# Gate and up projections of a feed-forward layer by seven half products instead of eight, with weight sums formed by accumulating loads

## The chip, the cores and the metric

The kernel runs on one core of a Trainium2 chip. The metric is the device time of one execution in microseconds (us). Three runs of the kernel before took 2762.12, 2761.25 and 2759.31 us; their median, 2761.25 us, is the time before.

## The reference

A trunk of two layers works on 512 tokens of width 1024. Each layer is a half-step feed-forward block, a token mixer with four branches, and a second half-step feed-forward block, each between two RMS norms:

```
def swiglu(h, w_gate, w_up, w_down):
    return (jax.nn.silu(h @ w_gate) * (h @ w_up)) @ w_down
...
for l in range(DEPTH):
    f = swiglu(rms_norm(h, ffn1_pre_g[l]), ffn1_w_gate[l], ffn1_w_up[l], ffn1_w_down[l])
    h = h + FFN_RESIDUAL_SCALE * rms_norm(f, ffn1_post_g[l])
    u = rms_norm(h, mix_pre_g[l])
    ...
    h = h + rms_norm(merged @ w_o[l], mix_post_g[l])
    f = swiglu(rms_norm(h, ffn2_pre_g[l]), ffn2_w_gate[l], ffn2_w_up[l], ffn2_w_down[l])
    h = h + FFN_RESIDUAL_SCALE * rms_norm(f, ffn2_post_g[l])
```

D_FF is 2816, so gate and up are each 1024 x 2816. All values are float32.

## The kernel before

**Numbers in two parts.** Every matrix operand is cut into a high part (a cast to float32r) and a low part (the rest), and a product of two such operands is three matmuls, high by high, high by low and low by high: `mm3` (L128 to L132) where a 128x128 block of weights is the stationary operand, `by_tokens` (L219 to L221) where the tokens are.

**The weights.** All weights lie in DRAM in one stream `ws`, in the order of their use, in chunks of eight 128x128 blocks (512 KB). `load` (L91 to L102) brings a chunk: a DMA on SP's queue into `raw` (3 buffers), ScalarE's cast to `wh` (L100), VectorE's subtraction to `wl` (L101). `block` hands out the next block of the stream and sees to it that the AHEAD = 3 chunks behind it are asked for.

**A feed-forward block.** `boundary` (L235) ends the block before and begins this one. It runs the last projection of the block before (down or output projection, tokens as stationary operand, result `py` in PSUM), and for each 128 tokens `gained` (squares on ScalarE, L233; product with the gain, L299), `update` (the residual stream `h`, held in SBUF, L304) and `normed` (squares, a power on GpSimd, L229; scaling to `u`, L250). `turned` transposes `u` (L262) and cuts it into `xh` and `xl` (L153, L146), for 256 tokens at a time. As soon as the first 256 tokens are there, `outer` multiplies them with 32 blocks of weights, two gate columns and two up columns (a column is 128 of the 2816 outputs) into four banks of PSUM `pf`; then the second 256 tokens follow with the same blocks. A third pair of columns is done by `group` (eight `mm3` of all 512 tokens in one bank).

`ffn` (L355) then takes each of the 22 column pairs: silu of gate (ScalarE, L361), times up (VectorE, L366), cut into `gh` and `gl` (L151, L144). The columns from the fourth on are dense: 8 blocks times 3 matmuls of 512 tokens for gate, and the same for up.

```
for f in range(3, KF):
    x = gate(group([(f"ffn{n}_w_gate", l, k, f * P) for k in range(KD)], xs))
    up(group([(f"ffn{n}_w_up", l, k, f * P) for k in range(KD)], xs), x)
```

**What sets the order.** Every engine works through its own instructions in order, and each has one queue of them. The kernel's order of calls, and the buffers that its pools have (8 banks of PSUM, 5 chunks each of `wh` and `wl`, 59 slots of 128x512 in SBUF), decide what stands where.

Of the kernel before, what the change touches and what calls it, by code (L numbers as in the profile page):

```python
# [9 lines left out]
F32 = mybir.dt.float32  # L10
F32R = mybir.dt.float32r
# [4 lines left out]
P = 128  # L16
# [22 lines left out]

PACE = (3, 1, 5)  # L40

HOLD = 8

_VECS = ("ffn1_pre_g", "mix_pre_g", "ffn2_pre_g", "a_conv_w", "b_conv_w", "b_conv_b", "b_ln_g", "b_ln_b", "c_subln_g")
# [10 lines left out]
def build(tc, ws, x, vecs, gains, wdf, lamv, fb, consts, out):  # L55
# [2 lines left out]
    order = []  # L58
    with ExitStack() as ctx:
        cp = ctx.enter_context(tc.tile_pool(name="cp", bufs=1))  # L60
        sp = ctx.enter_context(tc.tile_pool(name="sp", bufs=59))
        rawp = ctx.enter_context(tc.tile_pool(name="rawp", bufs=3))
        wp = ctx.enter_context(tc.tile_pool(name="wp", bufs=5))
        mp = ctx.enter_context(tc.tile_pool(name="mp", bufs=4))
        np_ = ctx.enter_context(tc.tile_pool(name="np", bufs=4))
        gp = ctx.enter_context(tc.tile_pool(name="gp", bufs=1))
# [21 lines left out]

        ready = {}

        def load(c, parts=1):  # L91
# [12 lines left out]
        def block(desc):  # L104
            i = len(order)
            order.append(desc)
            if i % CB == 0:
                c = i // CB
                for n in range(c, min(c + AHEAD + 1, NBLK // CB) if len(order) > 4 * KD else 0):
                    if n not in ready:  # L110
# [14 lines left out]
            for _ in range(min(pace[0], len(spare))):  # L125
                spare.pop(0)()

        def mm3(out, w, x, first, last):  # L128

            PE.matmul(out=out, lhsT=w[0], rhs=x[0], start=first, stop=False)  # L130
            PE.matmul(out=out, lhsT=w[0], rhs=x[1], start=False, stop=False)  # L131
            PE.matmul(out=out, lhsT=w[1], rhs=x[0], start=False, stop=last)  # L132

        def group(descs, xs):
            out = ps()
# [99 lines left out]
        def boundary(post, pre, first):  # L235
# [2 lines left out]


            xs, pf, blk = [], [], []  # L240
            stat = np_.tile([P, 16], F32, tag="stat", name=nm("stat"))

            def normed(t):

                for c in range(2):
                    squares(hs[t][c], stat[:, 8 + 2 * t + c:9 + 2 * t + c])
                r = rstd_of([stat[:, 8 + 2 * t + c:9 + 2 * t + c] for c in range(2)])
                us = [slot(F32, "u") for _ in range(2)]
                for c in range(2):
                    V.tensor_scalar(out=us[c], in0=hs[t][c], scalar1=r, scalar2=None, op0=ALU.mult)  # L250
                return us

            def turned(us, h):

                c = HALVES[h]
                for b in range(4):
                    p = ps("pt")
                    for i in range(2):
                        k = 2 * b + i
                        for t in range(2):  # L260
                            o = k % 4 * P
                            PE.transpose(out=p[:, i * H + t * P:i * H + (t + 1) * P],  # L262
                                         in_=us[t][k // 4][:, o:o + P], identity=ident)
                    for i in range(2):
                        k = 2 * b + i
# [4 lines left out]
                        lo_of(xs[k][1][:, c], p[:, i * H:(i + 1) * H], xs[k][0][:, c], g)  # L270

            def outer(k, c):

# [9 lines left out]
            if post is None:  # L283
                for t in range(4):
                    for c in range(2):
                        nc.sync.dma_start(out=hs[t][c], in_=x[t * P:(t + 1) * P, c * T:(c + 1) * T])
                    load(t, 2 if t == 0 else 1)
                us = [normed(t) for t in range(4)]
            else:
                row, factor, name, l, ys = post  # L290
                n = len(ys)
                gb = gp.tile([P, D], F32, tag="gb", name=nm("gb"))
                nc.scalar.dma_start(out=gb, in_=gains[row:row + 1, :].broadcast_to([P, D]))
                yg = [[None, None] for _ in range(4)]

                def gained(t, c, p):
                    squares(p, stat[:, 2 * t + c:2 * t + c + 1])
                    yg[t][c] = slot(F32, "yg")
                    V.tensor_mul(out=yg[t][c], in0=p, in1=gb[:, c * T:(c + 1) * T])  # L299
# [10 lines left out]
                settle()  # L310
                py = [ps("py") for _ in range(4)]
                for k in range(n):
                    w = tile4(name, l, k, 0)
# [23 lines left out]
                    return None  # L337
            if post is None:
                turned(us[0:2], 0)
            for k in range(KD - 2):  # L340
                outer(k, HALVES[0])
            turned(us[2:4], 1)
            for k in range(KD - 2, KD):
                outer(k, HALVES[0])
            for k in range(KD):
                outer(k, HALVES[1])
            pf.append(group(first[4], xs))
            pf.append(group(first[5], xs))
            return xs, pf


        def ffn_first(l, n):
            return [[(f"ffn{n}_w_{w}", l, k, f * P) for k in range(KD)] for f in range(3) for w in ("gate", "up")]

        def ffn(l, n, entry):  # L355
            xs, pf = entry
            gs = []

            def gate(pg):
                x = slot()  # L360
                S.activation(out=x, in_=pg, func=AF.Silu)  # L361
                return x

            def up(pu, x):
                u = slot()
                V.tensor_mul(out=u, in0=pu, in1=x)  # L366
                gs.append(split(u, s="g"))

            for f in range(3):
                x = gate(pf[2 * f])  # L370
                up(pf[2 * f + 1], x)
# [3 lines left out]
            settle()  # L375
            return 3 * l + 2 * n - 2, 0.5, f"ffn{n}_w_down", l, gs


        def cols(l, c0):
# [5 lines left out]
        def mixer(l, entry):  # L385
            lam_init = 0.8 - 0.6 * math.exp(-0.3 * l)
            xs, pf = entry

            def proj(c0):
                return group(cols(l, c0), xs)  # L390
# [357 lines left out]

        vec = cp.tile([P, NCOLS], F32, name="vec")
        nc.scalar.dma_start(out=vec, in_=vecs)  # L750
        hs = [[cp.tile([P, T], F32, name=f"h{t}{c}") for c in range(2)] for t in range(NQ)]
# [15 lines left out]
        qlo, nq = [[cp.tile([P, T], F32R, name=f"qlo{i}{m}") for m in range(2)] for i in range(2)], [0]  # L767
        for pair in qlo:
            for m in range(2):
                V.memset(pair[m][LANES[1 - m]].bitcast(F32), 0.0)  # L770
        mhalf = cp.tile([P, 4], F32, name="mhalf")
        V.memset(mhalf, -0.5)

# [67 lines left out]
```

## Time and profile before

| | |
|---|---|
| median of 3 runs | 2761.25 us (2759.31 to 2762.12) |
| the profiled execution | 2762.7 us, of which the span of its records is 2760.9 us |
| mean granted clock of TensorE | 0.995 |
| busy | TensorE matmuls 2717.1 us, VectorE 1392.6, ScalarE 980.1, GpSimd 71.5 |

The span is the time from the first to the last record; the rest of the execution's time lies around it. The profile has a line per engine of how busy it was, the chain of work that ended last, groups of like instructions with their mean duration, a timeline with the start of every instruction, and windows, which sum up a stretch. A row of the timeline or of the groups begins with the engine and the line of the source. TensorE appears twice: PE for matmuls and PEld for the loading of their stationary operand. The busy time of a matmul overlaps with that of the next, so the pace of matmuls is read from the distance of their starts and not from their duration.

### The profile page before, as it was taken

The numbers are of one execution on the slowest core, as the hardware profiler recorded it, in microseconds if no ns is written. First come the engines' busy times: TensorE is split into PE (matmuls) and PEld (weight loads), VectorE is DVE, ScalarE is ACT, GpSimd is POOL, SyncE is SP. The second block draws the span as 40 slices with busy tenths as digits, with TensorE's granted clock in tenths as the row PEclk, the third lists the DMA queues.
The fourth block names the chain that finished last, engine by engine and source line by source line (L and its number), as shares of the span: only waits on it lengthen the run. The fifth ranks groups of instructions, "written<-read, shape, count | busy, mean of one in ns | idle before, by whom it ended". The sixth has DMA issues, their size and how long they took to land.

```text
span 2760.9 us, 32249 instructions
## 1 busy us (share of the span) xinstructions
PE 2717.1 (98%) x12884; PEld 2274.7 (82%) x12884; DVE 1392.6 (50%) x2287; ACT 980.1 (35%) x1607; POOL 71.5 (3%) x114
## 2 busy tenths in 40 slices
PE   7999999999999999999999999999999999999998
PEld 6888888887888888888888888888878888888887
DVE  4333248777776453332353332596777854533322
ACT  4222232354454333222242222424545533432221
POOL 0000000000000000000000000000000000000000
PEclk9999999999999999999999999999999999999999
DMA  4222223222222222222222222222222222222221
GB/s 154 99 96 95 100 82 111 85 77 69 96 81 92 99 92 99 92 99 100 84 101 99 99 94 98 95 98 79 75 85 88 87 93 94 90 100 99 99 92 69
DMA packets 73494, 257.82 MB, mean 93 GB/s; under 512 B 8432, under 2 KB 8816, under 8 KB 73344
## 3 DMA queue, kind: packets, MB, share of 16 engines
q1 hardware_dynamic: 68688, 246.45, 25.7%
q10 hardware_dynamic: 4656, 9.32, 1.1%
q8 instruction: 101, 1.65, 0.2%
q14 instruction: 49, 0.40, 0.0%
HBM read 253.60 MB, written 2.13 MB: 93 GB/s over the span
## 4 chain that ended last, share of the span: by engine, by line
PE 95%; DVE 2%; ACT 1%; issue 1%; DMA 1%; POOL 1%; POOLq 0%; DVEq 0%; ACTq 0%
PE p L130 21%; PE p L132 21%; PE p L131 21%; PE py L219 6%; PE py L220 6%; PE py L221 6%; PE pf L131 2%; PE pf L132 2%; PE pf L130 2%; PE o L548 1%; PE pv L219 1%; PE pv L220 1%; PE pv L221 1%; PE pt L532 1%; PE sc L502 1%; DVE wl L101 1%
## 5 line engine op out<-in xcount | busy, mean ns | idle before, releaser
L100 ACT CAST wh<-raw 128x1024 fp32r<-128x1024 f32 (+1 forms) x465 | 488.7, 1051 | 1400.7 <-PE p L131 663.5
L101 DVE TENSOR_TENSOR wl<-raw,wh 128x1024 fp32r<-128x1024 f32 (+1 forms) x465 | 567.9, 1222 | 753.2 <-ACT wh L100 741.4
L130 PE MATMUL p<-xh,wh 128*128 128x512 f32 x2304 | 903.5, 392 | 0.0
L132 PE MATMUL p<-xh,wl 128*128 128x512 f32 x2304 | 898.4, 390 | 0.0
L131 PE MATMUL p<-xl,wh 128*128 128x512 f32 x2304 | 898.0, 390 | 0.0
L132 PEld LDWEIGHTS p<-xh,wl 128*128 128x128 f32 x2304 | 433.2, 188 | 90.8
L131 PEld LDWEIGHTS p<-xl,wh 128*128 128x128 f32 x2304 | 433.7, 188 | 89.1 <-issue 0.5
L130 PEld LDWEIGHTS p<-xh,wh 128*128 128x128 f32 x2304 | 433.8, 188 | 88.7 <-PE pt L532 0.5
L219 PE MATMUL py<-wh,gh 128*128 128x512 f32 x704 | 274.1, 389 | 0.0
L221 PE MATMUL py<-wh,gl 128*128 128x512 f32 x704 | 273.9, 389 | 0.0
L220 PE MATMUL py<-wl,gh 128*128 128x512 f32 x704 | 273.9, 389 | 0.0
L366 DVE TENSOR_TENSOR s<-p,s 128x512 f32<-128x512 f32 x80 | 55.3, 692 | 270.9 <-PE p L132 270.9
L395 DVE SCALAR_TENSOR_TENSOR yc<-ba,vec,yc 128x501 f32<-128x501 f32 (+17 forms) x240 | 170.0, 733 | 2.4
L221 PEld LDWEIGHTS py<-wh,gl 128*128 128x128 f32 x704 | 132.2, 188 | 27.6
L219 PEld LDWEIGHTS py<-wh,gh 128*128 128x128 f32 x704 | 132.2, 188 | 27.5
L220 PEld LDWEIGHTS py<-wl,gh 128*128 128x128 f32 x704 | 132.2, 188 | 27.1
L131 PE MATMUL pf<-xl,wh 128*128 128x256 f32 x384 | 112.8, 295 | 8.8 <-DVE xl L146 8.8
L130 PE MATMUL pf<-xh,wh 128*128 128x256 f32 x384 | 109.7, 296 | 4.4 <-ACT xh L153 3.1
L132 PE MATMUL pf<-xh,wl 128*128 128x256 f32 x384 | 112.2, 294 | 0.0
L522 ACT ACTIVATE e<-e,mx 128x128 f32<-128x128 f32 (+3 forms) x128 | 71.4, 558 | 66.1 <-DVE mx L520 54.4
L131 PEld LDWEIGHTS pf<-xl,wh 128*128 128x128 f32 x384 | 77.9, 203 | 10.1 <-DVE xl L146 10.1
L130 PEld LDWEIGHTS pf<-xh,wh 128*128 128x128 f32 x384 | 74.8, 200 | 7.9 <-ACT xh L153 5.6
(185 smaller groups left out, 2617.8 us busy)
## 6 DMA issues: line engine op xcount, KB each, us to landing
raw<-ws SPq DMA_DIRECT2D x463, 512.0 KB, 3.2
cb<-cum ACTq DMA_DIRECT2D x16, 256.0 KB, 3.5
gb<-gains ACTq DMA_DIRECT2D x6, 512.0 KB, 3.7
h<-x SPq DMA_DIRECT2D x8, 256.0 KB, 5.8
out<-h SPq DMA_DIRECT2D x4, 256.0 KB, 2.0
out<-h ACTq DMA_DIRECT2D x4, 256.0 KB, 2.0
raw<-ws SPq DMA_DIRECT2D x2, 256.0 KB, 7.1
cst<-consts ACTq DMA_DIRECT2D x1, 384.0 KB, 4.7
```

The source lines that it names most:

```text
L100: S.copy(out=wh[:, j], in_=raw[:, j])
L101: V.tensor_sub(out=wl[:, j], in0=raw[:, j], in1=wh[:, j].bitcast(F32))
L130: PE.matmul(out=out, lhsT=w[0], rhs=x[0], start=first, stop=False)
L131: PE.matmul(out=out, lhsT=w[0], rhs=x[1], start=False, stop=False)
L132: PE.matmul(out=out, lhsT=w[1], rhs=x[0], start=False, stop=last)
L219: PE.matmul(out=out, lhsT=x[0][:, r], rhs=w[0], start=first, stop=False)
L220: PE.matmul(out=out, lhsT=x[0][:, r], rhs=w[1], start=False, stop=False)
L221: PE.matmul(out=out, lhsT=x[1][:, r], rhs=w[0], start=False, stop=last)
L366: V.tensor_mul(out=u, in0=pu, in1=x)
L395: V.scalar_tensor_tensor(out=acc[:, s:], in0=y[:, :T - s], scalar=vcol(wname, l, i * 4 + j), in1=acc[:, s:], op0=ALU.mult, op1=ALU.add)
L502: PE.matmul(out=p[:, :n], lhsT=q[0][m][:, c], rhs=k[m][:, :n], start=True, stop=False)
L522: S.activation(out=e, in_=e, func=AF.Exp, scale=-1.0, bias=mx, accum_out=sums)
```

## The change

**Seven products for eight.** Of each feed-forward block, two column pairs stay as they were (through `outer`); the third, dense pair goes. The other 20 column pairs are taken in 10 groups (GROUPS) of two pairs. For gate and for up apart, the two columns (rows of the output) by 8 blocks of weights and by 512 tokens are seen as a 2x2 matrix of weights (a11, a12, a21, a22: two columns by the upper and lower four blocks of the 1024) times a 2x2 matrix of activations (b11 ... b22: upper and lower four blocks by the two halves of the tokens). By Strassen's scheme in Winograd's form the product takes seven products of sums instead of eight products: a12 b21, a11 b11, s1 nt1, s2 nt2, s3 t3, a22 t4 and s4 b22. Each is 4 blocks x 3 matmuls of 256 tokens, for gate and for up.

**The sums of weights.** `seven` (new, L466) loads the four quarters of a group. s1 to s4 are made by DMAs on GpSimd's queue that add to what lies in SBUF: `add` (L483). X receives s1, s2 and s4 in turn (three additions), Y receives s3 (one); Z and W are a12 and a22 as they are. An addition can begin when the cut of the sum before (cast and subtraction, `cut`, L104 and L105) has read the buffer. `raw` has 7 buffers now.

**The sums of activations.** In `boundary`, ScalarE keeps `xf`, the uncut second half (L294), GpSimd puts the first half together again from `xh` and `xl` (`whole`, L301), and VectorE makes nt1, nt2, t3 and t4 from them (`quarter_sums`, L417), each cut in two (`form`, L161 to L170).

**The sums of products.** Products add up in PSUM in banks f0 and f1. What two outputs share is copied out by ScalarE (`taken`, L499) and added by VectorE (`added`, L504).

**Residual stream in DRAM.** `normed` stores `h` by DMAs on ScalarE's queue (L268), and `fetch` reads gain and `h` back in the middle of the next projection (L330, L333). The cut of `g` in two parts moves from `ffn` into that projection (`part`). `qlo` is allotted and set to zero in each mixer.

```diff
-        sp = ctx.enter_context(tc.tile_pool(name="sp", bufs=59))
-        rawp = ctx.enter_context(tc.tile_pool(name="rawp", bufs=3))
+        sp = ctx.enter_context(tc.tile_pool(name="sp", bufs=65))
+        rawp = ctx.enter_context(tc.tile_pool(name="rawp", bufs=7))
...
             def normed(t):
                 for c in range(2):
                     squares(hs[t][c], stat[:, 8 + 2 * t + c:9 + 2 * t + c])
+                    if post is not None:
+                        nc.scalar.dma_start(out=hd[t][c], in_=hs[t][c])
...
+                    for i in range(2 if sums and h else 0):
+                        S.activation(out=xf[b][h][:, i * H:(i + 1) * H], in_=p[:, i * H:(i + 1) * H], func=AF.Copy,
+                                     scale=vcol(pre[0], pre[1], 2 * b + i))
...
             turned(us[2:4], 1)
...
+            for k in range(KD):
+                outer(k, HALVES[1])
+                if k == 0:
+                    nt1 = quarter_sums(ALU.subtract, b11, b12)
+                    form("nt1", nt1)
+                if k == 2:
+                    t2 = quarter_sums(ALU.add, b22, nt1)
+                    form("nt2", t2, True)
+                if k == 4:
+                    form("t3", quarter_sums(ALU.subtract, b22, b12))
+                if k == 6:
+                    form("t4", quarter_sums(ALU.subtract, t2, b21))
+                if k < 6:
+                    next(steps)
+            return steps, pf
...
+            def add(g, key, u):
+                G.dma_start(out=ga[g][key], in_=ws[base + 4 * g + u], accum_op=ALU.add)
...
+            def product(g, name, to, x, first):
+                wh, wl = ga[g].pop(name)
+                for i in range(2):
+                    for k in range(4):
+                        c = slice(i * T + k * P, i * T + (k + 1) * P)
+                        mm3(to[i], (wh[:, c], wl[:, c]), forms[x][k], first and k == 0, k == 3, True)
...
+                if r == -1:
+                    split_of(g, "a12", "Z")
+                    split_of(g, "s1", "X")
+                    add(g, "X", 0)
+                if r == 0:
+                    split_of(g, "a11", "Y")
+                    add(g, "Y", 2)
+                if r == 3:
+                    split_of(g, "s2", "X")
+                    add(g, "X", 1)
+                if r == 5:
+                    split_of(g, "s3", "Y")
...
+                if r == 2:
+                    d["f1"] = [ps("f1") for _ in range(2)]
+                    product(g, "a11", [p[:, HALVES[0]] for p in d["f1"]], "b11", True)
+                    taken(g, "n1")
+                    added(g, *[[p[:, HALVES[0]] for p in d["f0"]]] * 2, "n1")
+                if r == 3:
+                    product(g, "s1", [p[:, HALVES[1]] for p in d["f0"]], "nt1", True)
...
         def ffn(l, n, entry):
-            for f in range(3, KF):
-                x = gate(group([(f"ffn{n}_w_gate", l, k, f * P) for k in range(KD)], xs))
-                up(group([(f"ffn{n}_w_up", l, k, f * P) for k in range(KD)], xs), x)
+            steps, pf = entry
+            for f in range(2):
+                up(pf[2 * f + 1], gate(pf[2 * f]))
+            for t in steps:
...
```

**Where instructions stand.** Of two tensors with the same name, the number behind the underscore tells them apart; the rest of a row is line, operation, output, inputs and shape. ScalarE, before, where the second feed-forward block of the first layer begins; the first silu (L361) is the one that frees a bank `pf`:

```order
L153 ACTIVATE xh_8054<-pt_8225,vec 128x256
L153 ACTIVATE xh_8067<-pt_8234,vec 128x256
L153 ACTIVATE xh_8080<-pt_8243,vec 128x256
L100 CAST wh_8187<-raw_8186 128x1024
L100 CAST wh_8253<-raw_8252 128x1024
L100 CAST wh_8380<-raw_8379 128x1024
L361 ACT_TABLE_LOAD
L361 ACTIVATE s_8440<-pf_8122 128x512
L100 CAST wh_8411<-raw_8410 128x1024
L151 CAST gh_8444<-s_8442 128x512
```

Three casts of weights stand between the last cut of activations and the table load.

The same place now; `th` are the high parts of the sums of activations, `wh_9679` is s2, `wh_9713` s3, `wh_9746` and `wh_9750` a12 and s1 of the second group:

```order
L104 CAST wh_9679<-raw_9471 128x1024
L170 ACTIVATE th_9508<-t_9501 128x512
L104 CAST wh_9713<-raw_9512 128x1024
L168 CAST th_9542<-t_9538 128x512
L104 CAST wh_9746<-raw_9709 128x1024
L168 CAST th_9546<-t_9539 128x512
L104 CAST wh_9750<-raw_9677 128x1024
L168 CAST th_9592<-t_9588 128x512
L168 CAST th_9596<-t_9589 128x512
L452 ACT_TABLE_LOAD
L452 ACTIVATE s_9612<-pf_9297 128x512
L452 ACTIVATE s_9616<-pf_9299 128x512
```

The table load and the first silu (L452 now) stood behind three casts of weights; they now stand behind the cuts of all four sums of activations and of s2, s3 and the next group's first two.

TensorE now, at the end of a11's product of the first group (f_9647). f_9789 is the first bank of the second group, the ninth bank to be asked for; f_9646 gets s2, f_9620 s1:

```order
L149 MATMUL f_9647<-xh_9219,wl_9572 128x256
L147 MATMUL f_9789<-xh_9228,wh_9746 128x256 [waits PE_49,Activation_49]
L148 MATMUL f_9789<-xl_9229,wh_9746 128x256
L149 MATMUL f_9789<-xh_9228,wl_9747 128x256 [waits DVE_49]
L147 MATMUL f_9789<-xh_9232,wh_9746 128x256
L147 MATMUL f_9646<-th_9504,wh_9679 128x256 [waits Activation_49]
L148 MATMUL f_9646<-tl_9505,wh_9679 128x256
L149 MATMUL f_9646<-th_9504,wl_9680 128x256
L147 MATMUL f_9646<-th_9504,wh_9679 128x256
L147 MATMUL f_9620<-th_9463,wh_9554 128x256 [waits DVE_49]
```

The first product of the second group stands ahead of s2 and s1 of the first, and its first matmul waits for ScalarE.

GpSimd now, at the same boundary; nr_9281 is the power for the last 128 tokens, raw_9471 is X, raw_9512 Y:

```order
L246 TENSOR_TENSOR nr_9281<-nw_9280,mhalf 128x1
L301 TENSOR_TENSOR xf_8832<-xh_9202,xl_9203 128x256
L301 TENSOR_TENSOR xf_8832<-xh_9206,xl_9207 128x256
L301 TENSOR_TENSOR xf_8834<-xh_9215,xl_9216 128x256
L301 TENSOR_TENSOR xf_8834<-xh_9219,xl_9220 128x256
L301 TENSOR_TENSOR xf_8836<-xh_9228,xl_9229 128x256
L301 TENSOR_TENSOR xf_8836<-xh_9232,xl_9233 128x256
L301 TENSOR_TENSOR xf_8838<-xh_9241,xl_9242 128x256
L301 TENSOR_TENSOR xf_8838<-xh_9245,xl_9246 128x256
L483 DMA raw_9471<-ws 128x1024
L483 DMA raw_9512<-ws 128x1024
L483 DMA raw_9471<-ws 128x1024
```

The second addition to X (raw_9471, which makes s2) and the one to Y stand behind the eight additions that put `xf` together.

## Rows read from the trace of the kernel before

**Rows 1.** The page: share of the span by engine, and the chain of work that ended last.

```profile
PE 2717.1 (98%) x12884; PEld 2274.7 (82%) x12884; DVE 1392.6 (50%) x2287; ACT 980.1 (35%) x1607; POOL 71.5 (3%) x114
...
PE 95%; DVE 2%; ACT 1%; issue 1%; DMA 1%; POOL 1%; POOLq 0%; DVEq 0%; ACTq 0%
```

**Rows 2.** Windows, inside the first feed-forward block: the stretch, its length, then busy time and instructions of each engine, granted clock, share of the DMA engines.

```profile
110.00:340.00 230.00, 230.00 (x1016) 190.51 (x1015) 73.59 (x78) 63.63 (x81) 0.00 (x0) 1.00 0.28 96
```

**Rows 3.** Timeline of TensorE there: start, duration. Between the two rows lie 25 more matmuls of this form.

```profile
199.25 0.39 PE L130 MATMUL p<-xh,wh 128*128 128x512 f32 x1
...
205.14 0.39 PE L132 MATMUL p<-xh,wl 128*128 128x512 f32 x1
```

**Rows 4.** Timeline of TensorE, matmuls of 256 tokens in `outer`: 50 more lie between the first two rows, 9 between the last two.

```profile
405.62 0.29 PE L132 MATMUL pf<-xh,wl 128*128 128x256 f32 x1
...
411.73 0.28 PE L132 MATMUL pf<-xh,wl 128*128 128x256 f32 x1
...
1026.32 0.41 PE L132 MATMUL pf<-xh,wl 128*128 128x256 f32 x1
...
1028.45 0.41 PE L130 MATMUL pf<-xh,wh 128*128 128x256 f32 x1
```

**Rows 5.** Groups of like instructions on VectorE and ScalarE: busy time in all, mean ns of one, then idle time before them.

```profile
L101 DVE TENSOR_TENSOR wl<-raw,wh 128x1024 fp32r<-128x1024 f32 x463 | 566.5, 1224 | 750.4 <-ACT wh L100 738.6 <-PE pt L532 0.8 <-PE st L188 0.3
L100 ACT CAST wh<-raw 128x1024 fp32r<-128x1024 f32 x463 | 487.5, 1053 | 1397.1 <-PE p L131 663.5 <-issue 337.7 <-PE py L221 314.2
L569 DVE TENSOR_TENSOR s<-s,s 128x512 f32<-128x512 f32 x48 | 33.1, 690 | 1.2
L366 DVE TENSOR_TENSOR s<-p,s 128x512 f32<-128x512 f32 x80 | 55.3, 692 | 270.9 <-PE p L132 270.9
L144 DVE TENSOR_TENSOR gl<-s,gh 128x512 fp32r<-128x512 f32 x88 | 59.6, 685 | 0.0
L144 DVE TENSOR_TENSOR pl<-pt,ph 128x256 fp32r<-128x256 f32 x24 | 10.0, 415 | 0.0
L151 ACT CAST ph<-pt 128x256 fp32r<-128x256 f32 x24 | 9.1, 378 | 6.0 <-PE pt L532 6.0
L151 ACT CAST gh<-s 128x512 fp32r<-128x512 f32 x88 | 54.7, 621 | 3.5 <-DVE s L366 3.5
L361 ACT ACTIVATE s<-p 128x512 f32<-128x512 f32 x80 | 47.0, 588 | 0.0
L361 ACT ACT_TABLE_LOAD x3 | 3.8, 1283 | 0.1
```

**Rows 6.** DMA queues (packets, MB, share of 16 engines' span) and issues (count, KB each, median us from issue to landing); in the last row, of SP's issues, the shortest, median and longest ns of one.

```profile
q1 hardware_dynamic: 68688, 246.45, 25.7%
...
raw<-ws SPq DMA_DIRECT2D x463, 512.0 KB, 3.2
cb<-cum ACTq DMA_DIRECT2D x16, 256.0 KB, 3.5
...
L99 SPq DMA_DIRECT2D raw<-ws x465: 327/328/432, 1.7 to 2712.9; - x155
```

**Rows 7.** Timeline at the boundary before the second feed-forward block of the first layer: start, duration, in brackets the idle time before and what ended it.

```profile
1024.13 0.39 PE L131 MATMUL pf<-xl,wh 128*128 128x256 f32 x1 [1.47 <-DVE xl L146]
...
1034.01 0.55 POOL L229 TENSOR_TENSOR nr<-nw,mhalf 128x1 f32<-128x1 f32 x1 [2.60 <-DVE nw L228]
...
1036.75 2.67 ACT L153 ACTIVATE xh<-pt,vec 128x256 fp32r<-128x256 f32 x7 [3.07 <-PE pt L262]
...
1037.45 0.36 PE L130 MATMUL pf<-xh,wh 128*128 128x256 f32 x1
...
1040.89 0.48 DVE L146 SCALAR_TENSOR_TENSOR xl<-pt,vec,xh 128x256 fp32r<-128x256 f32 x1 [0.54 <-ACT xh L153]
...
1048.79 1.28 ACT L361 ACT_TABLE_LOAD   x1
1050.08 0.60 ACT L361 ACTIVATE s<-pf 128x512 f32<-128x512 f32 x1
```

**Rows 8.** Windows of that boundary, columns as in rows 2: behind the wait of TensorE, and the last stretch of `outer`.

```profile
1026.10:1028.60 2.50, 2.50 (x13) 2.50 (x13) 1.52 (x4) 1.61 (x4) 0.00 (x0) 0.50 0.64 228
1037.40:1049.00 11.60, 11.60 (x99) 11.60 (x98) 5.91 (x11) 5.84 (x11) 0.00 (x0) 1.00 0.21 66
```

**Rows 9.** Groups on GpSimd, columns as in rows 5.

```profile
L512 POOL CAST ph<-zeros 128x128 fp32r<-128x128 f32 x24 | 15.4, 640 | 565.5 <-DVE s L448 206.7 <-PE o L548 101.5 <-DVE s L569 74.6
L577 POOL CAST w8s<-zeros 128x192 fp32r<-128x192 f32 x2 | 1.1, 546 | 0.0
```

More of the change, by code (lines that the diff above doesn't have):

```diff
@@ L89, in build, with cut @@
         ready = {}
+        apart = set()
+        for l in range(DEPTH):
+            for n in range(2):
+                c = (2 * FFN_CHUNKS + MIX_CHUNKS) * l + (FFN_CHUNKS + MIX_CHUNKS) * n + PLAIN
+                apart.update(range(c, c + 4 * GROUPS))
+        def cut(raw):
+            wh = wp.tile([P, CB * P], F32R, tag="wh", name=nm("wh"))
+            wl = wp.tile([P, CB * P], F32R, tag="wl", name=nm("wl"))
+            S.copy(out=wh, in_=raw)
+            V.tensor_sub(out=wl, in0=raw, in1=wh.bitcast(F32))
+            return wh, wl
         def load(c, parts=1):
@@ L109, in block @@
                 for n in range(c, min(c + AHEAD + 1, NBLK // CB) if len(order) > 4 * KD else 0):
-                    if n not in ready:
+                    if n not in ready and n not in apart:
                         load(n)
@@ L126, in cover, with mm3 @@
                 spare.pop(0)()
[L128 to L132, printed above, removed]
+        def mm3(out, w, x, first, last, free=False):
+            PE.matmul(out=out, lhsT=w[0], rhs=x[0], start=first, stop=False, skip_group_check=free)
+            PE.matmul(out=out, lhsT=w[0], rhs=x[1], start=False, stop=False, skip_group_check=free)
+            PE.matmul(out=out, lhsT=w[1], rhs=x[0], start=False, stop=last, skip_group_check=free)
         def group(descs, xs):
@@ L240, in boundary @@
             xs, pf, blk = [], [], []
+            sums = pre is not None and pre[0] != "mix_pre_g"
+            xf = [[slot(F32, "xf") for _ in range(2)] for _ in range(4)] if sums else None
+            hs = [[None, None] for _ in range(NQ)]
             stat = np_.tile([P, 16], F32, tag="stat", name=nm("stat"))
@@ L291, in boundary, with fetch, part @@
                 n = len(ys)
-                gb = gp.tile([P, D], F32, tag="gb", name=nm("gb"))
-                nc.scalar.dma_start(out=gb, in_=gains[row:row + 1, :].broadcast_to([P, D]))
+                gb = []
+                def fetch():
+                    for c in range(2):
+                        gb.append(slot(F32, "gb"))
+                        nc.scalar.dma_start(out=gb[c], in_=gains[row:row + 1, c * T:(c + 1) * T].broadcast_to([P, T]))
+                        for t in range(NQ):
+                            hs[t][c] = slot(F32, "h")
+                            nc.scalar.dma_start(out=hs[t][c], in_=hd[t][c] if row else
+                                                x[t * P:(t + 1) * P, c * T:(c + 1) * T])
+                def part(k):
+                    if k < n and not isinstance(ys[k], tuple):
+                        ys[k] = halves(ys[k])
                 yg = [[None, None] for _ in range(4)]
@@ L342, in boundary, with form, quarter_sums @@
             turned(us[2:4], 1)
+            if not sums:
+                for k in range(KD - 2, KD):
+                    outer(k, HALVES[0])
+                for k in range(KD):
+                    outer(k, HALVES[1])
+                pf.append(group(first[4], xs))
+                pf.append(group(first[5], xs))
+                return xs, pf
+            forms, t2 = {}, [None, None]
+            def form(name, srcs, negate=False):
+                out = []
+                for src in srcs:
+                    hi, lo = slot(F32R, "th"), slot(F32R, "tl")
+                    hi_of(hi, src, -1.0 if negate else None)
+                    lo_of(lo, src, hi, -1.0 if negate else None)
+                    out.extend((hi[:, i * H:(i + 1) * H], lo[:, i * H:(i + 1) * H]) for i in range(2))
+                forms[name] = out
+            def quarter_sums(op, a, b):
+                out = [slot(F32, "t") for _ in range(2)]
+                for i in range(2):
+                    V.tensor_tensor(out=out[i], in0=a[i], in1=b[i], op=op)
+                return out
+            b11, b12, b21, b22 = ([xf[b + 2 * r][h] for b in range(2)] for r in range(2) for h in range(2))
+            for j, k in enumerate(range(4)):
+                forms.setdefault("b11", []).append(tuple(v[:, HALVES[0]] for v in xs[k]))
+                forms.setdefault("b21", []).append(tuple(v[:, HALVES[0]] for v in xs[k + 4]))
+                forms.setdefault("b22", []).append(tuple(v[:, HALVES[1]] for v in xs[k + 4]))
+            steps = seven(first[0][0][0], first[1][0][0], first[0][0][1], forms)
             for k in range(KD - 2, KD):
@@ new lines, in boundary @@
+                if k == 2:
[8 more added lines that the diff above has]
+            return steps, pf
+        def ffn_first(l, n):
+            return [[(f"ffn{n}_w_{w}", l, k, f * P) for k in range(KD)] for f in range(2) for w in ("gate", "up")]
@@ new lines, in build, with gate, up, halves @@
+        gs = []
+        def gate(pg, scale=1.0):
+            x = slot()
+            S.activation(out=x, in_=pg, func=AF.Silu, scale=scale)
+            return x
+        def up(pu, x, scale=1.0):
+            u = slot(F32, "g")
+            V.scalar_tensor_tensor(out=u, in0=pu, scalar=scale, in1=x, op0=ALU.mult, op1=ALU.mult)
+            gs.append(u)
+        def halves(src):
+            hi, lo = slot(F32R, "gh"), slot(F32R, "gl")
+            hi_of(hi, src)
+            lo_of(lo, src, hi)
+            return hi, lo
@@ new lines, in ffn @@
+        def ffn(l, n, entry):
+            steps, pf = entry
+            for f in range(2):
+                up(pf[2 * f + 1], gate(pf[2 * f]))
+            for t in steps:
+                if t == 7 * GROUPS - 2:
+                    for k in range(AHEAD):
+                        gs[k] = halves(gs[k])
+                if t >= 7 * GROUPS + 2 and t % 2:
+                    c = len(order) // CB + (t - 7 * GROUPS - 2) // 2
+                    load(c)
+            ys = gs[:]
+            gs.clear()
+            return 3 * l + 2 * n - 2, 0.5, f"ffn{n}_w_down", l, ys
@@ L387, in mixer @@
             xs, pf = entry
+            qlo, nq = [[slot(F32R, "ql") for m in range(2)] for i in range(2)], [0]
+            for pair in qlo:
+                for m in range(2):
+                    V.memset(pair[m][LANES[1 - m]].bitcast(F32), 0.0)
             def proj(c0):
@@ L766, in build @@
         V.memset(zeros, 0.0)
[L767 to L770, printed above, removed]
         mhalf = cp.tile([P, 4], F32, name="mhalf")
```

96 lines of the change are left out of this document (74 added, 22 removed).

## The prediction

> **What bounds the kernel now.** I read the page first: PE is busy 98% of the span and makes up 95% of the chain, VectorE stands at 50%, ScalarE at 35% [rows 1]. So a stage gets shorter only if PE gets less to do there, and whatever makes PE wait costs its full length. Then the windows: in the middle of a feed-forward block PE has no gap in 230 us, VectorE works 73.6 us and ScalarE 63.6, and the DMA engines 28% [rows 2]. The timeline gives the pace of matmuls: with 512 tokens 26 starts in 5.89 us, 0.2265 us each [rows 3]; with 256 tokens 51 starts in 6.11 us, 0.1198 each, and 10 in 2.13 us, 0.213 each, where the clock is low [rows 4].
>
> **What PE saves.** Two dense column pairs were 96 matmuls of 512 tokens, 96 x 0.2265 = 21.75 us. A group is now 7 products x 2 x 4 blocks x 3 matmuls = 168 of 256 tokens, 168 x 0.1198 = 20.13 us. That is 1.62 us less for each of 10 groups in 4 blocks: **-64.8 us**. Seven for eight would be 2.72 us; a matmul of half the tokens takes 53% of the time, which eats 1.1 of it.
>
> **Where a group could be held up.** The cuts of seven chunks cost VectorE 7 x 1.224, the six copies' additions 6 x 0.415 and two products of some 0.69, 12.4 us in all; ScalarE 7 x 1.053 + 6 x 0.378 + 2 x 0.588 = 10.8 us [rows 5]. Both fit in 20.1 us. What counts is order. s1 adds to f0, and may start only when VectorE has added the copy of a11's first bank. That bank is ready 12 matmuls, 1.44 us, before a11 ends; the copy (0.378) and the addition (0.415) fit, unless ScalarE and VectorE are at s4's cut (1.053 and 1.224) then. With five buffers of `wh` a cast starts when the fifth before it has been used; s4's starts 2.9 us before a11 ends, and the addition is done 0.15 us before PE wants it. So the bounds of this wait are 0 and 1.6 us (all four in a row, less 1.44) per group.
>
> The weight sums are the other holder. A plain load of 512 KB keeps the 16 DMA engines for 25.7% x 2760.9 us x 0.524 / 246.45 = 1.51 us, and lands 3.2 us after its issue [rows 6]. An accumulating load isn't in the trace. It brings as many bytes, so 1.51 us is its lower bound; twice the landing time of a load, 6.4 us, is the upper one, if it first fetches what lies there and then goes over it again. I take twice a load, 3.0 us, as the row of one load is the nearest. A group then needs 4 x 1.51 + 4 x 3.0 = 18 us of DMA engines, of 20.1. The tightest sum is s2's: the next s1's cast may start when a22 has been used, 11.5 us into a group, its cut ends at 13.8, and s2's cast is due when s3 has been used, at 20.2; so 6.4 us are left for waiting on GpSimd, issue and landing. I put landing at 3.2 + 1.5 = 4.7 us and the issue at 0.3 (SP's, rows 6) to 1.7 us (a wide guess: three of GpSimd's small casts, rows 9). That just fits, so I take 0.3 us per group for both holders together, **+12 us**, bounds 0 and 1.6 x 40 = 64.
>
> [...]
>
> **The fill at each feed-forward block.** This is the largest loss I see. `outer`'s second half starts at 1037.45, its 96 matmuls take 11.5 us [rows 7, 8]; a12 and a11 add 2 x 24 x 0.12 = 5.8. So PE has work for 17.3 us. Its next instruction wants a ninth bank, which the first silu frees. Before, that silu stood behind three casts, ended at 1050.7, 13.2 us in [rows 7], and the dense third pair (48 x 0.2265 = 10.9 us) covered it. Now it stands behind the cuts of all the activation sums. VectorE gets to these when the last `xl` is done: 1041.4 before [rows 7], now after six copies of `xf` on ScalarE (0.378 each) at about 1042.6, 5.2 us in. Until the last of t4's sums it has 8 sums (0.690), 5 cuts of weights (1.224) and 6 low parts (0.685): 15.8 us [rows 5], so 21.0 us in. Then a high part (0.62), the table load (1.283) and silu (0.588): **23.5 us in, 6.2 us after PE ran dry**. Lower bound: even with VectorE out of the way, the cast ahead of it (the next group's s1) needs a11's buffer, free at 17.3, so silu comes 4.2 us late. On top, s2's addition stands on GpSimd behind eight additions of 128 x 256. These start at 1034.6 [rows 7]; GpSimd's cast of 128 x 128 took 0.64 and 128 x 192 0.55 [rows 9], so I put one at 1.3 us (bounds 0.6, and 2.6 for twice the width and two inputs), done 7.6 us in; the sum then lands 13 us in, about 1 us after VectorE could use it. [...] Together 6.2 + 0.3 for handovers + 1 + 1.5 = 9 us, four times: **+36 us** (bounds 17, from 4.2 each, and 78, with 2.6 us an addition). The first block, which has no projection ahead of it, I take like the others.
>
> [...]
>
> **The small parts.** In the first half of each such boundary a fifth chunk (a12) is cut between the `xh` and `xl` that PE waits for: 1.2 us of VectorE, four times, **+5** (0 to 10). `normed` issues eight stores on ScalarE at five boundaries; at 0.33 us an issue [rows 6] only the last group's count, **+2** (0 to 13). The loads of gain and `h`, ten on ScalarE, and the cuts of `g`, 22 x 0.62 on ScalarE and 22 x 0.685 on VectorE, lie in the down projection, where PE has 59.8 us of matmuls (264 x 0.2265) for its first half alone: nothing. Zeroing `qlo` lies in the mixer, nothing. The last products of a block alternate on PE with the down projection's first: nothing, at most 1 us each.
>
> **Sum.** 2762.7 - 64.8 + 12 + 36 + 5 + 2 = 2752.9 us for an execution like the profiled one, which lies 1.45 above the median: **2751.5 us**, 0.35% faster. I take 0.2%, 5.5 us, as what a measurement can tell.
>
> **Rivals.** (A) *The fill is at its lower bound* and groups run without a wait: 2762.7 - 64.8 + 17 - 1.4 = 2714 us. For it: VectorE is half idle there before [rows 8], and a sum that lands early costs nothing. Against it: 15.8 us of VectorE's own durations don't shrink. (B) *The sums are late in every group*, the case on the other side. From 6.7 us between the end of s1's cut and landing, each further us costs 1 us in each of 40 groups, since ScalarE and VectorE stand in order behind the waiting cast, s1's addition among the rest. At 8 us it is 1.6 x 40 = 64 where I took 12: 2803. The same place with another cause: above (20.1 - 6.0) / 4 = 3.5 us of engine time per accumulating load the DMA engines become the bound, and at 4.5 us a group takes 24.0 us, 2.3 more than before, and the kernel 2761 + 40 x 2.3 + 43 = 2896. For it: 90% load of the DMA engines by my own estimate, and 6.4 us against 5 to 6.4; against it, the rows have no accumulating load that is slow. (C) *GpSimd's additions take 2.6 us each*: they end 18 us in, s2's sum lands 23 in, silu comes 10 us later than in my sum; 4 x 10.5 more with the clock, 2793. For it: GpSimd's rows are slow for their size [rows 9]. (D) *It saves nothing*, because matmuls of 256 tokens pace by their weight loads: 168 x 0.19 us would be 31.9 us a group, +406 us. Rows 4 show 0.12 with a load for each, so this is nearly out.
>
> **Chances.** Forecast, 2735 to 2768: 0.45 (0.34 faster, 0.11 no change). A: 0.18. B: 0.27. C: 0.09. D: 0.01. Faster 0.52, same 0.11, slower 0.37. From A's 2714 to B's 2803 lie about 8 in 10; I take 2712 to 2806. The forecast's own range is 2735 to 2768.
>
> **What will show it.** Right: groups 20.1 us apart; PE idle 6 to 9 us at each of four entries, released by the first silu's bank; a low clock behind; DMA share near 0.9 within a block; SP's queue never late. Wrong: PE waiting for a sum's DMA through VectorE or ScalarE in every group (B); more than 1.5 us per addition on line 301 (C); DMA share at 0.6 or less, with loads of 1.5 us, or no idle at the entries (A).

## The result and the profile after

The changed kernel takes 2723.35 us (four runs, 2720.78 to 2726.98) against 2760.94 (four runs of the kernel before, 2759.31 to 2762.12): **37.6 us less**, a ratio of 0.9865 with a 95% interval of 0.9848 to 0.9882. The forecast was 2751.5, faster by 9.8. The sign was right, and the time lies in the wide range (2712 to 2806) but not in the forecast's own (2735 to 2768). The gain is four times what the sum gave, so most of the work below is on what the sum left out.

The page of the profile after, engines and DMA queues; the rows answer to [rows 1, 6]:

```profile
PE 2659.3 (98%) x15764; PEld 2363.5 (87%) x15764; DVE 1658.8 (61%) x2715; ACT 1204.7 (44%) x2031; POOL 233.9 (9%) x306
...
q1 hardware_dynamic: 68688, 246.45, 26.7%
q0 software_dynamic: 23040, 83.90, 17.5%
...
raw<-ws POOLq DMA_DIRECT2D x160, 512.0 KB, 5.6
```

q0 carries the accumulating loads: 17.5% of 2720.1 us over 160 loads is 2.98 us of the DMA engines each, the 3.0 that the prediction took; a plain one takes 26.7% x 2720.1 x 0.524 / 246.45 = 1.54. One lands 5.6 us after its issue.

A window inside the second feed-forward block, and ScalarE's silus there (as [rows 2, 3] for the dense columns):

```profile
1062.00:1240.00 178.00, 178.00 (x1469) 177.06 (x1468) 106.75 (x136) 91.74 (x136) 26.77 (x31) 1.00 0.83 204
```

```profile
1127.63 0.59 ACT L452 ACTIVATE s<-f 128x512 f32<-128x512 f32 x1
...
1208.92 0.59 ACT L452 ACTIVATE s<-f 128x512 f32<-128x512 f32 x1
```

PE has no gap, the DMA engines are at 83%. From the first to the last of these rows lie four groups: 81.29 / 4 = 20.32 us each, where 20.13 was forecast without waits and 21.75 is two dense pairs. In the other three blocks the first silus of successive groups stand 20.3 us apart as well, but for a few gaps of 20.5 to 21.7.

The entry of that block (as [rows 7]); first PE, then ScalarE and VectorE:

```profile
1020.22 0.36 PE L148 MATMUL pf<-xl,wh 128*128 128x256 f32 x1
...
1037.69 0.28 PE L149 MATMUL f<-xh,wl 128*128 128x256 f32 x1
1044.46 0.58 PE L147 MATMUL f<-xh,wh 128*128 128x256 f32 x1 [6.49 <-ACT s L452]
...
1033.06 1.05 ACT L104 CAST wh<-raw 128x1024 fp32r<-128x1024 f32 x1 [1.94 <-DMA raw<-ws]
...
1043.81 1.08 ACT L452 ACTIVATE s<-pf 128x512 f32<-128x512 f32 x2
...
1034.14 1.23 DVE L105 TENSOR_TENSOR wl<-raw,wh 128x1024 fp32r<-128x1024 f32 x1 [2.30 <-ACT wh L104]
```

PE runs dry 17.8 us after the second half's start (17.3 forecast), and the first silu is done 24.2 us after it (23.5, and 24.8 with handovers and the late sum). The two waits at 1033 and 1034 are those for s2's sum. PE's waits over the whole execution (us in all, times, longest), and windows of 7.54 us behind each of the four waits for the first silu:

```profile
PE f L147 <- ACT s L452: 20.4, 4, 6.5
PE pt L284 <- DVE u L272: 20.2, 5, 14.7
PE pf L148 <- DVE xl L163: 7.2, 6, 2.1
PE f L147 <- DVE f L504: 3.5, 5, 1.3
PE pf L147 <- ACT xh L170: 1.1, 1, 1.1
PE pt L745 <- DVE e L813: 0.3, 2, 0.2
```

```profile
58.96:66.50 7.54, 7.54 (x50) 7.54 (x51) 3.17 (x5) 1.91 (x4) 0.86 (x1) 0.77 0.69 159
1044.46:1052.00 7.54, 7.54 (x44) 7.54 (x45) 2.22 (x5) 2.31 (x5) 0.00 (x0) 0.67 0.42 70
1405.03:1412.57 7.54, 6.89 (x35) 6.59 (x36) 3.00 (x6) 1.21 (x4) 0.86 (x1) 0.59 0.48 102
2391.88:2399.42 7.54, 7.54 (x41) 7.54 (x42) 1.94 (x4) 1.97 (x4) 0.00 (x0) 0.62 0.40 72
```

The four waits for the first silu make 20.4 us: 2.0 at the first block, 6.5, 5.4 and 6.5 at the others. At a granted clock of 0.77, 0.67, 0.59 and 0.62 behind them, some 10 us more are lost. The waits at the three later blocks and the low clock were forecast, if not to the digit. What was not forecast is in the last row of the waits: at the transposes of the mixer PE waits 0.3 us in all, and before it was this:

```profile
PE pt L532 <- DVE e L600: 8.7, 4, 2.2
```

And the chain behind it before, first VectorE, then PE, in the first mixer's fourth head:

```profile
661.33 0.42 DVE L520 CUSTOM_DVE_ANT_0 e<-sc,bias 128x256 f32<-128x256 f32 x1 [4.56 <-PE sc L502]
...
675.36 1.12 PE L532 MATMUL pt<-cst,e 128*128 128x128 f32 x4 [2.17 <-DVE e L600]
```

VectorE waits 4.56 us for scores, does its share late, and PE waits twice 2.17 us for it, the second time until 675.36; then comes this stretch, also of before, at a granted clock of 0.56:

```profile
674.40:681.40 7.00, 6.04 (x18) 4.95 (x19) 5.55 (x8) 1.44 (x4) 0.68 (x1) 0.56 0.44 150
```

### The profile page after: what moved, and what is told of

Its sections match the earlier page's. It is cut to its first block, busy times and chain, and to the rows that moved or that the text cites. A ratio compares the mean times of both kernels' runs of the same rounds, so it can differ in the third digit from the quotient of the medians.

```text
span 2720.1 us, 39646 instructions
## 1 busy us (share of the span) xinstructions
PE 2659.3 (98%) x15764; PEld 2363.5 (87%) x15764; DVE 1658.8 (61%) x2715; ACT 1204.7 (44%) x2031; POOL 233.9 (9%) x306
## 3 DMA queue, kind: packets, MB, share of 16 engines
q1 hardware_dynamic: 68688, 246.45, 26.7%
q0 software_dynamic: 23040, 83.90, 17.5%
## 5 line engine op out<-in xcount | busy, mean ns | idle before, releaser
L105 DVE TENSOR_TENSOR wl<-raw,wh 128x1024 fp32r<-128x1024 f32 x280 | 342.5, 1223 | 315.4 <-ACT wh L104 314.9
L104 ACT CAST wh<-raw 128x1024 fp32r<-128x1024 f32 x280 | 293.8, 1049 | 313.2 <-PE f L148 210.5
L147 PE MATMUL p<-xh,wh 128*128 128x512 f32 x1024 | 404.3, 395 | 0.0
L149 PE MATMUL p<-xh,wl 128*128 128x512 f32 x1024 | 399.4, 390 | 0.0
L148 PE MATMUL p<-xl,wh 128*128 128x512 f32 x1024 | 398.8, 389 | 0.0
L147 PE MATMUL f<-th,wh 128*128 128x256 f32 x1280 | 369.5, 290 | 3.5 <-DVE f L504 3.5
L148 PE MATMUL f<-tl,wh 128*128 128x256 f32 x1280 | 364.0, 285 | 0.0
L149 PE MATMUL f<-th,wl 128*128 128x256 f32 x1280 | 358.6, 285 | 0.0
L147 PE MATMUL f<-xh,wh 128*128 128x256 f32 x960 | 273.9, 285 | 20.4 <-ACT s L452 20.4
L148 PE MATMUL f<-xl,wh 128*128 128x256 f32 x960 | 273.0, 284 | 0.0
L483 POOL DMA_DIRECT2D raw<-ws x160 | 138.7, 867 | 1143.2 <-DMA raw<-ws 614.8
```

The costliest lines, as they stand in the source:

```text
L104: S.copy(out=wh, in_=raw)
L105: V.tensor_sub(out=wl, in0=raw, in1=wh.bitcast(F32))
L483: G.dma_start(out=ga[g][key], in_=ws[base + 4 * g + u], accum_op=ALU.add)
```

## The experiments

Each was run against the kernel before on its chip (2761.05 to 2761.86 there). The programs name the same slot of SBUF for that 128x256 of `e` and for the query's high part `qh` of the same head, which the scores of the last 128 rows still read: so these exponentials wait for scores that come after theirs. The changed kernel's mixer has 61 free slots (65 less four for `qlo`) where the kernel before had 59. That was the theory for the first three.

**Two slots more.** The pool has 61 slots; the boundary's gain, which had a buffer of its own, takes two of them, outside the mixer:

```diff
-        sp = ctx.enter_context(tc.tile_pool(name="sp", bufs=59))
+        sp = ctx.enter_context(tc.tile_pool(name="sp", bufs=61))
...
-                gb = gp.tile([P, D], F32, tag="gb", name=nm("gb"))
+                gb = [slot(F32, "gb") for _ in range(2)]
```

> The kernel before, with the gain of the boundary held in two slots of the common pool and that pool at 61 slots of 128x512 instead of 59; nothing else. Theory (slots): the changed kernel lost two waits of 2.17 us of TensorE and 6.8 us at the low clock in each mixer, at the transposes of the fourth head, because its mixer has two slots more (65 less 4 for the query's low parts, against 59), so that the exponentials no longer get slots that the same head's later scores still read. Then this kernel loses them too: 7 us in each of two mixers, 14 us less than before, some 2747 us, and no wait of TensorE for VectorE at those transposes. Rival (something else of the change freed the mixer, such as the query's low parts as pool slots or the residual stream out of SBUF): within 3 us of 2761, and the two waits stay.

2747.09 us, ratio 0.9951 (0.9938 to 0.9963): 14.0 less. PE's wait there, which was 8.7 us:

```profile
PE pt L532 <- DVE e L600: 0.4, 2, 0.2
```

**The same two slots taken from the changed kernel.**

```diff
-        sp = ctx.enter_context(tc.tile_pool(name="sp", bufs=65))
+        sp = ctx.enter_context(tc.tile_pool(name="sp", bufs=63))
```

> The changed kernel with 63 slots in the common pool instead of 65, so that the mixer has 59 as before. Theory (slots): the waits at the fourth head's transposes come back, 7 us in each mixer, 2723 + 14 = 2737. Rival (not the slots): 2723 within 3 us.

2737.25, ratio 0.9913 (0.9900 to 0.9927): 13.9 more than the changed kernel, and the wait is back:

```profile
PE pt L745 <- DVE e L813: 8.7, 4, 2.2
```

So the two slots are shown from both sides: adding them ends the wait and taking them brings it back.

**The residual part alone.** The changed kernel with dense feed-forward blocks:

```diff
-        sp = ctx.enter_context(tc.tile_pool(name="sp", bufs=65))
-        rawp = ctx.enter_context(tc.tile_pool(name="rawp", bufs=7))
+        sp = ctx.enter_context(tc.tile_pool(name="sp", bufs=73))
+        rawp = ctx.enter_context(tc.tile_pool(name="rawp", bufs=3))
...
-            sums = pre is not None and pre[0] != "mix_pre_g"
+            sums = False
```

> The residual part of the change alone: residual stream in DRAM, gain and low parts of the query in pool slots, 73 slots, feed-forward blocks dense as before, no sums. Theory (slots): the 14 us of the two mixers, less what the stores and loads cost, which I put at 2 us: some 2749. Theory (mixer and boundaries): the changed kernel's first halves of the boundaries show no low clock any more, 1.7 us at each of five; if that comes with the residual in DRAM, 8 us more: 2741. Rival (the residual part only costs): 2761 to 2774.

2739.65, ratio 0.9923 (0.9909 to 0.9936): 21.4 less, the second theory. **More than half of the gain is the residual part**, and the seven products add 2739.65 - 2723.35 = 16.3 us. Its mean granted clock is 1.00, where it was 0.995, and PE's waits for `xh` and `xl` are shorter, 8.3 us in all where they were 13.2. The next run asks what does that.

**The stores alone**, on top of the two slots; nothing reads them:

```diff
                 for c in range(2):
                     squares(hs[t][c], stat[:, 8 + 2 * t + c:9 + 2 * t + c])
+                    if post is not None:
+                        nc.scalar.dma_start(out=hd[t][c], in_=hs[t][c])
```

> The kernel before with 61 slots and the gain in two of them (2747), and the stores of the residual stream to DRAM on ScalarE's queue added, which nothing reads; the stream itself stays in SBUF. Theory (the stores shift ScalarE's order, so that a high part of the activations comes ahead of the last cut of weights and TensorE's wait at each boundary falls from some 1.9 to 1.1 us and leaves no low clock): 2740, as with the whole residual part. Rival (loads of the stream, or the slots, did that): 2747 to 2750.

2738.05, ratio 0.9915 (0.9901 to 0.9928): some 9 us less than without the stores. At the boundary before the second feed-forward block, without the stores, ScalarE and then PE's wait; below them the waits for `xl` over the whole execution and a window behind the wait at the first of the five boundaries, at a granted clock of 0.73:

```profile
1011.62 1.05 ACT L99 CAST wh<-raw 128x1024 fp32r<-128x1024 f32 x1 [0.61 <-ACT sq L232]
1012.58 0.46 ACT L152 ACTIVATE xh<-pt,vec 128x256 fp32r<-128x256 f32 x1
...
1015.17 0.39 PE L130 MATMUL pf<-xl,wh 128*128 128x256 f32 x1 [1.46 <-DVE xl L145]
...
PE pf L130 <- DVE xl L145: 8.4, 6, 1.5
...
392.00:398.00 6.00, 6.00 (x40) 6.00 (x40) 3.71 (x9) 2.61 (x7) 0.55 (x1) 0.73 0.33 113
```

and with them:

```profile
1009.38 0.46 ACT L152 ACTIVATE xh<-pt,vec 128x256 fp32r<-128x256 f32 x1
1010.08 1.05 ACT L99 CAST wh<-raw 128x1024 fp32r<-128x1024 f32 x1 [0.24 <-ACT xh L152]
...
1012.50 0.39 PE L130 MATMUL pf<-xl,wh 128*128 128x256 f32 x1 [1.03 <-DVE xl L145]
...
PE pf L130 <- DVE xl L145: 6.4, 6, 1.3
```

The first high part of the activations has moved ahead of a cast of weights, and `xl` comes sooner; the stores themselves do no work that anyone needs. At each of the five boundaries PE waits 1.7 to 2.0 us for `xh` and `xl` without the stores and 1.0 us with them. Behind three of the five the clock is at 0.73 to 0.77 in windows of 6 to 7 us without them, and at 1.00 with them. That is 4.3 us of waits and 4.7 of clock, the 9 us. The time is that of the whole residual part within 2 us, so neither its loads nor more slots than 61 are needed for it. That a reordering follows from the stores is shown; why the order falls out so when the program is built was not looked into.

**The first silu ahead of t3 and t4.**

```diff
+            for f in range(2):
+                up(pf[2 * f + 1], gate(pf[2 * f]))
+            form("t3", quarter_sums(ALU.subtract, b22, b12))
+            form("t4", quarter_sums(ALU.subtract, t2, b21))
             return steps, pf
```

> The changed kernel with the silu and product of the two column pairs of the boundary written ahead of the sums t3 and t4, all else alike. Theory (fill): TensorE's four waits for the first silu (20.4 us in all) and the 27 us at the low clock behind them (13.6 us lost) go; a wait of 1 to 2 us per block is left, since s3's cast still stands ahead of the silu and the copy of a11 behind it: 2723 - 34 + 6 = 2695. Rival (what comes next is as late): the wait moves to s1 or s3, whose sums of activations are now cut later, and TensorE waits as long there: 2723 within 6 us.

2721.88, ratio 0.9858 (0.9844 to 0.9871): nothing that can be told from 2723. The wait for the silu is gone, and others stand in its place; PE from 1020 to 1060:

```profile
PE f L147 <- ACT wh L104: 3.1, 2, 2.0
PE f L147 <- ACT n L499: 1.3, 1, 1.3
PE f L149 <- DVE wl L105: 1.2, 2, 0.6
```

5.6 us where it was 6.5; over the whole execution PE's waits in the seven products are 20.7 us where they were 23.9. My theory fell, the rival held: the silu was the last in a queue of work on VectorE and ScalarE, and whatever stands last there is waited for. If so, only more work for PE helps, or less for them.

**More work for PE**: two dense pairs again between the boundary's pairs and the groups, 9 groups:

```diff
-GROUPS = KF // 2 - 1
-PLAIN, FFN_CHUNKS, MIX_CHUNKS = 4, 3 * KD * KF // CB, 800 // CB
+GROUPS = KF // 2 - 2
+PLAIN, FFN_CHUNKS, MIX_CHUNKS = 8, 3 * KD * KF // CB, 800 // CB
...
+            pf.extend(group(first[f], xs) for f in range(4, 8))
             return steps, pf
```

> The changed kernel with two dense column pairs put back between the boundary's two pairs and the groups, so that 9 groups are left of 10 per block: 43.5 us more of matmuls that need no sum, while the sums of activations and weights are made. Theory (the fill is bounded by the cuts and sums on VectorE and by the first accumulating loads, and TensorE only lacks other work meanwhile): the waits at the entry (20.4 us) and the low clock behind them (13.6 us) go, and four groups are given up at 1.4 to 1.6 us each: 2723 - 34 + 6 = 2695. Rival (the wait moves along with the groups: the five buffers of cut weights are shared between dense chunks and the first products, so the sums are only cut when the dense chunks are done): the waits stay, 2723 + 6 = 2729.

2698.04, ratio 0.9770 (0.9757 to 0.9784): **25 us less than the changed kernel**, with fewer of the cheap products. The waits of 20.4 us and the 10 us of clock behind them, less 1.4 us for each of four groups given up, make 24.7. No wait for a silu is left among PE's, all of which are:

```profile
PE pt L284 <- DVE u L272: 20.3, 5, 14.3
PE pf L148 <- DVE xl L163: 8.3, 6, 1.9
PE f L147 <- DVE f L505: 4.2, 7, 1.3
PE pf L147 <- ACT xh L170: 1.6, 1, 1.6
PE pt L746 <- DVE e L814: 0.2, 1, 0.2
```

**Plain loads in place of the accumulating ones**, so the weights' sums are left out:

```diff
-                G.dma_start(out=ga[g][key], in_=ws[base + 4 * g + u], accum_op=ALU.add)
+                G.dma_start(out=ga[g][key], in_=ws[base + 4 * g + u])
```

> The changed kernel with the four accumulating loads of a group turned into plain loads on the same queue: the sums of weights are left out, all instructions stay. Theory (sums late): VectorE's and ScalarE's waits for the first sums at each entry (2.3 and 1.3 us) go, and the group's 0.2 us over its 20.16 too: 40 x 0.2 + 4 x 3 and some clock, 2723 - 22 = 2701. Rival (sums land in time, what holds a group is the order of copy and addition on ScalarE and VectorE): only the entry gains, 2723 - 8 = 2715 or above, and the group stays at 20.35.

2710.32, ratio 0.9815 (0.9801 to 0.9828): 13 less, between the two. The silus in a block, two rows four groups apart, the queue and PE's waits:

```profile
1120.79 0.59 ACT L452 ACTIVATE s<-f 128x512 f32<-128x512 f32 x1
...
1202.13 0.59 ACT L452 ACTIVATE s<-f 128x512 f32<-128x512 f32 x1
```

```profile
q0 software_dynamic: 23040, 83.90, 10.0%
...
raw<-ws POOLq DMA_DIRECT2D x160, 512.0 KB, 4.4
```

```profile
PE f L147 <- ACT s L452: 15.0, 4, 5.3
...
PE f L147 <- DVE f L504: 0.8, 1, 0.8
```

81.34 / 4 = 20.33 us a group, as with the sums: in the steady group the sums land in time, as the rival had it. Its other half, that the order of copy and addition holds the group, is not shown by this: all that can be seen is that four starts of PE in a group come 0.02 to 0.12 us late, at the same places in both traces. What the sums cost is at the entries (20.4 to 15.0), the late ones now and then (3.5 to 0.8), and the clock behind these. A plain load on this queue takes 10.0% x 2708.4 / 160 = 1.69 us of the DMA engines, an accumulating one 1.76 times that.

**More load on the DMA engines**: a12 and a22 loaded twice.

```diff
-                nc.sync.dma_start(out=ga[g][key], in_=ws[base + 4 * g + u])
+                for _ in range(2 if key in "ZW" else 1):
+                    nc.sync.dma_start(out=ga[g][key], in_=ws[base + 4 * g + u])
```

> The changed kernel with the plain loads of a12 and a22 issued twice into the same buffer: 3.1 us more of DMA work per group, nothing else. An accumulating load took 2.98 us of the 16 DMA engines and a plain one 1.54, so a group asks for 4 x 1.54 + 4 x 2.98 = 18.1 us of 20.35, and here for 21.2. Theory (the DMA engines are next to the bound): a group takes 21.2 us, 40 x 0.85 = 34 us more, 2757, with a DMA share near 1 inside the blocks. Rival (they could overlap more than the sum of the packets' times says): within 6 us of 2723.

2807.13, ratio 1.0159 (1.0145 to 1.0173): 84 more, not 34, and the share is not near 1. A window of this kernel, the accumulating loads in it, and who waited there:

```profile
1100.00:1250.00 150.00, 134.65 (x1067) 133.23 (x1066) 75.92 (x96) 64.29 (x97) 21.71 (x25) 0.95 0.87 227
```

```profile
raw<-ws POOLq DMA_DIRECT2D x25, 512.0 KB, 7.2
```

```profile
ACT wh L104 <- DMA raw<-ws: 38.3, 13, 6.5
...
PE f L147 <- DVE f L505: 15.4, 7, 3.9
```

Both theories were wrong on the way. The DMA engines didn't fill up first: their share in this window is 0.87. The accumulating loads landed after 7.2 us there; in the same window of the changed kernel it was 5.5, at 0.79. ScalarE's casts wait 38.3 us for loads there (7.5 in the changed kernel), and s1 waits for the addition behind the late cast in every group, just as rival B had it, with a clock of 0.95 on top.

**The additions of `xf` on VectorE**, in the kernel with cover:

```diff
-                    G.tensor_tensor(out=xf[k // 2][0][:, i * H:(i + 1) * H], in0=xs[k][0][:, HALVES[0]].bitcast(F32),
+                    V.tensor_tensor(out=xf[k // 2][0][:, i * H:(i + 1) * H], in0=xs[k][0][:, HALVES[0]].bitcast(F32),
...
-            whole()
             for k in range(KD - 2):
                 outer(k, HALVES[0])
             turned(us[2:4], 1)
+            whole()
```

> The kernel with two dense pairs as cover (2698), and the eight additions that put the first half of the activations together moved from GpSimd to VectorE, behind the second half's transposes. Theory (GpSimd's additions run beside VectorE's last scalings u and slow them: 1.81 us for two there, against 0.88 in the kernel before, so that TensorE waits 1.2 to 1.5 us for u at three entries): u is back at 0.88, the wait falls to 0.5 or less, three times 0.9 us, 2695; the eight additions on VectorE, 8 x 0.415 = 3.3 us, are covered. Rival (the wait comes from the accumulating load that GpSimd issues ahead of the power, or VectorE's 3.3 us come too early): 2698 to 2703.

2697.63 (2693.34 to 2698.13), ratio 0.9768 (0.9755 to 0.9782): the expected 3 us are too few to tell it from 2698.04. The lengthening of `u` is seen in the traces, though. The last two scalings `u` with the additions on GpSimd, and the additions:

```profile
1015.11 1.81 DVE L272 TENSOR_SCALAR u<-h,nr 128x512 f32<-128x512 f32 x2 [0.73 <-POOL nr L246]
...
1015.05 5.93 POOL L301 TENSOR_TENSOR xf<-xh,xl 128x256 f32<-128x256 f32 x8
```

and without them on GpSimd:

```profile
1014.96 0.88 DVE L272 TENSOR_SCALAR u<-h,nr 128x512 f32<-128x512 f32 x2 [0.73 <-POOL nr L246]
```

PE's waits for `u` at the three later entries fell from 1.2 to 1.5 us to 0.8 to 0.9, not to the 0.5 that was expected: the additions are a part of them, and what the rest is was not found.

## Why the prediction was right and wrong

That the time lies in the wide range, next to rival A's 2714, is luck: neither A's reasons nor the forecast's brought it there. With the seven products alone, 16.3 us, it would be about 2745, inside the forecast's own range; the other 21.4 us are of a part that the sum has at +2.

The seven products with their entries, groups and extra cuts were put at -64.8 + 12 + 36 + 5 = -11.8 us. Alone, on top of the residual part, they measure -16.3. By steps:

- *What PE saves, and the groups' waits*: -52.8 in the sum. 40 groups of 20.32 for 21.75 us make -57.2, and PE's waits for s1's addition give 3.5 back: -53.7. The size is right. The 0.19 us by which a group is over its 20.13 stay when the sums are left out, so they are not the sums; the 3.5 fall to 0.8 then, so most of them are.
- *The fill*: +36. Measured 20.4 us of waits and some 10 us of clock behind them, about 30. No run shows the 1.5 us that the sum has for the clock behind each wait; in its place the four windows of 7.54 us give an estimate of 1.7 to 3.1 us each, from their clocks of 0.77 to 0.59. The mechanism, its place and, at the three later blocks, its length (5.4 to 6.5 us where 7.2 to 7.5 was forecast) were right; taking the first block like the others was not, it waited 2.0. What I had not seen is that it is a whole queue's length and not the silu's place: moving the silu gained nothing, giving PE other work gained 25 us.
- *The fifth chunk's cut*: +5. PE's waits for `xh` and `xl` are 8.3 us, as with the residual part alone. Instead PE waits for `u` at the three later entries, 1.1 to 1.3 us each, which the sum did not have: 20.2 us for `u` in all, against 16.5 with the residual part alone. These three steps add up to -19.6 us; what the 3 us up to -16.3 are was not found.
- *Chances*: A's lower bound of 4.2 us was met at none of the three later entries (at the first the wait was 2.0, below it), B's and C's prices weren't reached. An addition on GpSimd took 0.73 us (1.3 in the sum).
- *The accumulating load*: put at twice a load, 3.0 us. It took 2.98 us against 1.54 for a plain one on SP's queue, 1.94 times, and against 1.69 on the same queue, 1.76 times.

**The step that failed is the small parts**: "Zeroing `qlo` lies in the mixer, nothing", and the stores at +2. I priced what the residual part issues and moves, and found it hidden. I did not ask what it frees. It takes 21.4 us off: 14 in the mixers, where two more slots end a wait on a reused buffer, and some 7 to 9 at the boundaries, where the stores shift ScalarE's order. Both stood in the profile before: 8.7 us of PE's waits at the mixer's transposes, with the clock low behind them, and a wait of 1.47 us with the clock low at a boundary [rows 7, 8]. A row of the waits that no term of the sum touches was a reason to ask what ends it.

## What to carry to other kernels

When a change moves buffers, price what it frees as well as what it issues: list the waits of the bounding engine in stages that the change doesn't aim at, and ask of each whether a buffer's earlier owner ends it. A pipeline that needs sums or cuts before its first product needs other work for the bounding engine as long as that preparation takes; keep some of the plain form for it, since reordering the preparation only moved the wait here (20.7 us in all where it was 23.9). And test a change of several parts by its parts: here the part that looked like bookkeeping made more than half of the gain.

## What the runs showed of the hardware

An accumulating load of 512 KB took 2.98 us of the DMA engines and landed in 5.6 us (4.4 for a plain one on the same queue); with the engines at 0.87 in the run with more loads it landed in 7.2. Two scalings of 128x512 on VectorE, from SBUF to SBUF, took 1.81 us beside GpSimd's additions and 0.88 without them. So VectorE's instructions were lengthened by 0.9 us over the two, with GpSimd's additions at 0.73 us each; by what means was not shown.
